# A 2048-wide trunk on one core: the whole down product of the MLP by seven-product slabs, its halves taking turns on the PSUM banks

## The chip, the core and the metric

The kernel runs on one core of a Trainium2 chip. The core has a matrix engine (TensorE, PE in the profile, with its weight loads shown as PEld), three elementwise engines (VectorE = DVE, ScalarE = ACT, GpSimd = POOL) and a queue engine for transfers (SyncE = SP). They run side by side and wait for each other only through semaphores. The metric is device time in microseconds (us) for one execution; the number of a kernel is the median of its timed runs.

## The reference

Two decoder layers over 256 tokens of width 2048, all in float32. What this change touches is the MLP that ends each layer, with `w_ff1` 2048 x 8192 and `w_ff2` 8192 x 2048:

```python
def squared_relu_mlp(h, w1, w2):
    z = jax.nn.relu(h @ w1)
    return (z * z) @ w2

# in each of the two layers, after the attention part
x = x + squared_relu_mlp(rms_norm(x, ffn_norm[i]), w_ff1[i], w_ff2[i])
```

Before the first MLP stand a pooling mixer and a memory attention, between the two MLPs the shared keys and values and a differential attention. None of that is changed.

## The kernel before

**Numbers.** A float32 factor is split in two parts that TensorE multiplies at full rate: a high part (ScalarE rounds, "cast") and a low part (VectorE subtracts the high part from the number). A product takes high x high, high x low and low x high. Weights are read from DRAM in rows of 128 x 1024 numbers (`raw`, `slab`), and every row has to go through one cast on ScalarE (L171) and one subtraction on VectorE (L174) before TensorE may use it. The split parts stand in a ring of six places of 512 columns (`hi_ring`, `lo_ring`), with two more in the MLP (`slot`); a place is free again when TensorE has used it. `Feed` does this: at each use it prepares up to `AHEAD = 3` jobs further, as far as places are free (`fill`, `_slots`).

**Plain tiles.** The up product has 64 output tiles of 128 columns ("f 0" to "f 63"), each summed over 16 blocks of K. `narrow` runs one: per block a 512-column matmul with the weights' high part (L893) and a 256-column one with the low part (L895). Two weight rows feed one tile. `up_tile` copies the finished bank to SBUF (L907), and after every second tile `convert` makes the squared-ReLU pair: eight small steps on VectorE and ScalarE, each put some quarter tiles later by `at(d, fn)`. The results are z (high and low part) and four sums and differences of z's blocks, all kept in `za` and `zb`.

**Slabs.** The second half of the down product's columns (1024 to 2047) isn't run by tiles. For each pair of K blocks, `slab_jobs(i)` runs a 2 x 2 block product with seven products in place of eight. A slab reads two rows (`ra`, `rb`; VectorE also makes one difference, L202, and one sum over 1024 columns, L205; a GpSimd transfer adds a third piece to `ra` while it lands, L142). It is split in four jobs of 2, 1, 2 and 2 products; a product is three 512-column matmuls (L977 to L979) into a PSUM bank of its own. So a slab has 21 matmuls, and the seven sums stay open in seven of the eight banks over all 32 slabs of a layer. Meanwhile all plain tiles use the one bank left (`x_bank`). When the last slab is done, `finish_banks` combines the seven banks into four blocks (two copies on ScalarE, seven additions on VectorE, L999 to L1007), scales them (L1010) and turns them with 16 transposes of TensorE (L1019).

**The first half** of the down product's columns (0 to 1023) runs by plain tiles ("d q n": quarter q of K, column block n), 32 per layer, each with three VectorE steps after it (`add_down`, L913 to L915).

**Order.** `tiles` lists the plain tiles; `slab_plan` puts slab jobs into the gaps between them, one slab to about three gaps. Then a scheduler orders each engine's instructions.

Of the kernel before, what the change touches and what calls it, by code (L numbers as in the profile page):

```python
# [18 lines left out]
P = 128  # L19
T = 256  # L20
# [8 lines left out]
DOWN = 36  # L29
# [254 lines left out]
def slab_plan(tiles):  # L284
# [11 lines left out]
    gaps = {}  # L296
    t = ready[0]
    for i in range(32):
        t = max(t, ready[i])
        groups = ((0,), (1, 2), (3,))  # L300
        late = i - sum(ready[k] <= t for k in ready)
        if late < -2 or t > len(tiles) - 12:
            groups = ((0, 1), (2, 3))
        if tiles[t] == ("d", 3, 0):
            groups = ((0, 1, 2, 3),)
        for g in groups:
            gaps[t] = [(i, j) for j in g]
            t += 1
    return gaps
# [27 lines left out]
def program(ctx, tc, plan, dry, xT, memT, par, lam, cst, wst, yT):  # L337
# [6 lines left out]
    pp = ctx.enter_context(tc.tile_pool(name="pp", bufs=1, space=PSUM))  # L344

# [46 lines left out]
    resid = sp.tile([P, NK, T], F32, name="resid")  # L392
# [411 lines left out]
    def ffn(l, xs, tag, done):  # L804

        ZS, SS = 22, 5
# [12 lines left out]
        made = [-1]  # L819
        whole = [0]  # L820
        ran = [0]
        downs = [0]

        def zs(j, n=1):
            s = j % ZS
            t, s = (za, s) if s < NK else (zb, s - NK)
            return t[:, s : s + n, :]

        def z(j):
            return zs(j)[:, 0, :]  # L830

        def sit(i):
            s = ZS - NK + 2 * (i % SS)
            return zb[:, s : s + 2, :].rearrange("p a c -> p (a c)")
# [4 lines left out]
        def convert(i, late):  # L839
# [16 lines left out]
            def high():  # L856
                assert dry or (2 * i < ZS or downs[0] >= 8 * ((2 * i + 1 - ZS) // NK + 1)), i
                nc.scalar.copy(zs(2 * i, 2)[:, :, 0:T], u)

            def low():  # L860
                whole[0] = 2 * i + 2
                zz = zs(2 * i, 2)
# [9 lines left out]
            def sums_high():  # L872
                assert dry or ran[0] > i - SS, i
                nc.scalar.copy(sit(i)[:, 0:512].rearrange("p (a c) -> p a c", a=2), sums)

            def sums_low():
                h, l = (sit(i)[:, c : c + 512].rearrange("p (a c) -> p a c", a=2) for c in (0, 512))
                nc.vector.tensor_sub(l, sums, h.bitcast(F32))
                made[0] = i
# [5 lines left out]
        def narrow(ps, w, n, ks, src):  # L885
            for j in range(0, len(ks), 2):
# [4 lines left out]
                assert dry or w == "w_ff1" or whole[0] > ks[j + 1]  # L891
# [9 lines left out]
        def up_tile(j, ps):  # L901
# [6 lines left out]
            if j % 2:  # L908
                convert(j // 2, (1, 1, 2, 2, 3, 4, 5, 6) if j == 63 else (1, 2, 3, 4, 6, 7, 8, 10))
# [7 lines left out]
        def down_tile(q, n, ps):  # L917
            ks = list(range(q * NK, q * NK + NK))
            if l == 1 and q == 3 and n == 7:
# [11 lines left out]
                tick()  # L931
                rest = douts[(downs[0] + 1) % 2][:, 0:T]
# [4 lines left out]
            narrow(ps, "w_ff2", n, ks, z)  # L937
            dout = douts[downs[0] % 2]
# [731 lines left out]
```

## Time and profile before

| | |
|---|---|
| timed runs | 2038.71 us median of 3 (2038.3 to 2039.28) |
| the profiled execution's own time | 2039.43 us, span of the profile 2037.7 us |
| PE / PEld busy | 2031.2 us (100%) / 1746.1 us (86%) |
| DVE / ACT / POOL busy | 1626.4 us (80%) / 1322.8 us (65%) / 109.8 us (5%) |
| granted TensorE clock | 1.000 over the whole span |
| HBM | 201 GB/s on average |
| MLP of layer 0, of layer 1 | about 255 to 943 us, about 1341 to 2033 us of the span |

A row of the page's groups reads: line, engine, operation, output<-inputs, sizes, count | busy time, mean duration of one | idle time before it and who ended it. In the timeline a row is start, duration, engine, line and operation; matmuls overlap, so what one costs is the distance from one start to the next.

### The profile page before, as it was taken

The numbers are of one execution on the slowest core, as the hardware profiler recorded it, in microseconds if no ns is written. First come the engines' busy times: TensorE is split into PE (matmuls) and PEld (weight loads), VectorE is DVE, ScalarE is ACT, GpSimd is POOL, SyncE is SP. The second block draws the span as 40 slices with busy tenths as digits, with TensorE's granted clock in tenths as the row PEclk, the third lists the DMA queues.
The fourth block names the chain that finished last, engine by engine and source line by source line (L and its number), as shares of the span: only waits on it lengthen the run. The fifth ranks groups of instructions, "written<-read, shape, count | busy, mean of one in ns | idle before, by whom it ended". The sixth has DMA issues, their size and how long they took to land.

```text
span 2037.7 us, 30955 instructions
## 1 busy us (share of the span) xinstructions
PE 2031.2 (100%) x11088; PEld 1746.1 (86%) x11088; DVE 1626.4 (80%) x2529; ACT 1322.8 (65%) x2105; POOL 109.8 (5%) x131
## 2 busy tenths in 40 slices
PE   9999999999999999999999999999999999999999
PEld 7888888888888888888888899888888888888887
DVE  8888778877877777789775798877877777787787
ACT  7765566666655656669665698566666656665664
POOL 0001300000000000000000000310000000000000
PEclk9999999999999999999999999999999999999999
DMA  9565666776766666766656645657676766667764
GB/s 310 177 201 190 195 191 200 209 222 198 217 210 198 216 203 202 216 186 205 210 186 191 193 142 177 193 174 216 203 222 200 217 198 207 216 198 213 209 203 145
DMA packets 121835, 410.48 MB, mean 201 GB/s; under 512 B 13840, under 2 KB 16912, under 8 KB 121680
## 3 DMA queue, kind: packets, MB, share of 16 engines
q1 hardware_dynamic: 112320, 391.70, 59.6%
q0 software_dynamic: 9216, 16.78, 5.0%
q8 instruction: 87, 1.43, 0.3%
q14 instruction: 68, 0.56, 0.1%
q10 hardware_dynamic: 144, 0.01, 0.0%
HBM read 403.59 MB, written 2.10 MB: 199 GB/s over the span
## 4 chain that ended last, share of the span: by engine, by line
PE 99%; DMA 0%; DVE 0%; SPq 0%; ACT 0%; issue 0%; ACTq 0%
PE x_bank L893 32%; PE x_bank L895 16%; PE wo L488 6%; PE p L978 5%; PE p L977 5%; PE p L979 5%; PE ff L893 3%; PE wo L490 3%; PE q L519 3%; PE k L519 3%; PE v L519 3%; PE u L488 2%; PE mk L519 2%; PE mv L519 2%; PE ff L895 2%; PE u L490 1%
## 5 line engine op out<-in xcount | busy, mean ns | idle before, releaser
L171 ACT CAST hi_ring<-raw 128x512 fp32r<-128x512 f32 (+1 forms) x725 | 575.3, 799 | 351.3 <-PE x_bank L893 146.4
L174 DVE TENSOR_TENSOR lo_ring<-raw,hi_ring 128x512 fp32r<-128x512 f32 (+1 forms) x725 | 659.2, 917 | 173.4 <-ACT hi_ring L171 161.1
L174 DVE TENSOR_TENSOR lo_ring<-slab,hi_ring 128x1024 fp32r<-128x1024 f32 (+1 forms) x182 | 188.1, 1033 | 62.8 <-ACT hi_ring L171 53.7
L171 ACT CAST hi_ring<-slab 128x1024 fp32r<-128x1024 f32 (+1 forms) x182 | 163.9, 901 | 82.2 <-PE x_bank L893 43.5
L893 PE MATMUL x_bank<-fx,hi_ring 128*128 128x512 f32 x688 | 216.1, 395 | 0.0
L488 PE MATMUL wo<-cat,hi_ring 128*128 128x512 f32 x512 | 161.6, 396 | 0.0
L171 ACT CAST slot<-raw 128x1024 fp32r<-128x1024 f32 x84 | 88.3, 1051 | 106.5 <-PE x_bank L893 101.8
L895 PEld LDWEIGHTS x_bank<-fx,lo_ring 128*128 128x128 f32 x688 | 129.2, 188 | 30.2
L142 POOL DMA_DIRECT2D slab<-in_w x64 | 55.4, 865 | 1724.3 <-DMA slab<-in_w 1546.8
L174 DVE TENSOR_TENSOR slot<-raw,slot 128x1024 fp32r<-128x1024 f32 x84 | 103.2, 1229 | 51.1 <-ACT slot L171 51.0
L895 PE MATMUL x_bank<-fx,lo_ring 128*128 128x256 f32 x688 | 135.1, 278 | 0.0
L174 DVE TENSOR_TENSOR slot<-slab,slot 128x1024 fp32r<-128x1024 f32 x74 | 90.5, 1223 | 49.8 <-ACT slot L171 47.9
L893 PE MATMUL x_bank<-fx0a,hi_ring 128*128 128x512 f32 x368 | 115.7, 396 | 0.0
L490 PEld LDWEIGHTS wo<-cat,lo_ring 128*128 128x128 f32 x512 | 96.1, 188 | 22.0
L893 PEld LDWEIGHTS x_bank<-fx,hi_ring 128*128 128x128 f32 x688 | 107.6, 189 | 4.8 <-ACT room L907 1.6
L171 ACT CAST slot<-slab 128x1024 fp32r<-128x1024 f32 x74 | 77.8, 1051 | 50.2 <-PE x_bank L893 31.2
L490 PE MATMUL wo<-cat,lo_ring 128*128 128x256 f32 x512 | 101.7, 278 | 0.0
L893 PE MATMUL x_bank<-fx0b,hi_ring 128*128 128x512 f32 x320 | 100.5, 395 | 0.0
L893 PE MATMUL x_bank<-za,hi_ring 128*128 128x512 f32 x296 | 93.0, 395 | 0.0
L907 ACT COPY room<-x_bank 128x512 f32<-128x512 f32 x118 | 68.7, 582 | 35.9 <-PE x_bank L895 35.9
L895 PEld LDWEIGHTS x_bank<-fx0a,lo_ring 128*128 128x128 f32 x368 | 69.1, 188 | 16.0
L978 PE MATMUL p<-hi_ring,zb 128*128 128x512 f32 x210 | 82.1, 391 | 0.0
(494 smaller groups left out, 4836.8 us busy)
## 6 DMA issues: line engine op xcount, KB each, us to landing
raw<-in_w SPq DMA_DIRECT2D x596, 512.0 KB, 4.2
slab<-in_w SPq DMA_DIRECT2D x128, 512.0 KB, 3.4
slab<-in_w POOLq DMA_DIRECT2D x64, 256.0 KB, 4.8
resid<-in_x SPq DMA_DIRECT2D x8, 256.0 KB, 5.7
memraw<-in_mem SPq DMA_DIRECT2D x4, 512.0 KB, 3.7
out_y<-resid SPq DMA_DIRECT2D x16, 128.0 KB, 1.9
memraw<-in_mem SPq DMA_DIRECT2D x6, 256.0 KB, 6.2
qodd<-both SPq DMA_DIRECT2D x6, 256.0 KB, 3.5
```

The lines of the kernel that those rows point to most:

```text
L142: self.nc.gpsimd.dma_start(t[:, 512:1024], self.wst[other, :, 512:1024], accum_op=ALU.add)
L171: cast = self.nc.scalar.copy(hi, src)
L174: self.nc.vector.tensor_sub(lo, src, hi.bitcast(F32))
L488: nc.tensor.matmul(ps, hi, xs[:, k, :], start=first and j == 0, stop=False)
L490: nc.tensor.matmul(ps[:, T : 2 * T], lo, xs[:, k, 0:T], start=False, stop=last and j == len(ks) - 1,)
L519: nc.tensor.matmul(ps[t], a, b, start=i == 0 and j == 0, stop=i == NK - 1 and j == 2)
L893: nc.tensor.matmul(ps, hi, src(k), start=k == ks[0], stop=False)
L895: nc.tensor.matmul(ps[:, T : 2 * T], lo, src(k)[:, 0:T], start=False, stop=k == ks[-1])
L907: nc.scalar.copy(pairs[j // 2 % 3][:, 512 * (j % 2) : 512 * (j % 2) + 512], ps)
L977: nc.tensor.matmul(ps, al, hi[:, s], start=i == 0, stop=False)
L978: nc.tensor.matmul(ps, ah, hi[:, s], start=False, stop=False)
L979: nc.tensor.matmul(ps, ah, lo[:, s], start=False, stop=i == 31)
```

## The change

Both halves of the down product's columns now go through slabs. Half "A" is the old one (columns 1024 to 2047, all 32 slabs). Half "B" (columns 0 to 1023) takes the first 24 slabs, three quarters of K; the last quarter stays with the eight tiles "d 3 n". The tiles "d 0 n" to "d 2 n" are gone. Seven banks can hold only one half at a time, so the halves take turns: A slabs 0 to 6, B 0 to 13, A 7 to 20, B 14 to 23, A 21 to 31 (`PHASES`). At each turn `finish_banks` combines the seven banks; a sum that isn't whole is parked in a DRAM tile (`part`) and added back at the half's next turn by an accumulating transfer on GpSimd's queue. `ffn_plan` gives each tile credit for four slab jobs. z and its sums get their places from a list (`spots`), since both halves must have read a place before it is free. The second half of the residual stream is copied to a DRAM tile (`kept`) during the MLP, so that its SBUF could serve as two more places; the built program has no instruction that uses these.

```diff
+STEPS = (1, 2, 3, 4, 6, 7, 8, 10)
+NB = 24
+PHASES = (("A", 0, 7), ("B", 0, 14), ("A", 7, 21), ("B", 14, 24), ("A", 21, 32))
+RATE = 4.0
...
+def ffn_plan(tiles):
...
+    jobs = [(p, i, j) for p, (_, a, b) in enumerate(PHASES) for i in range(a, b) for j in range(4)]
+    items = []
+    credit = 0.0
+    phase = hold = 0
+    for t, what in enumerate(tiles):
+        credit = min(credit + RATE, 8.0)
+        if what == ("d", 3, 0):
+            credit = max(credit, 4.0)
+        while t >= hold and jobs and credit >= 1 and ready[jobs[0][1]] <= t:
+            p, i, j = jobs[0]
+            if p != phase:
+                items.append(("end", phase))
+                phase = p
+                hold = t + (4 if PHASES[p - 1][2] == NB else 1)
+                break
+            items.append(("s", *jobs.pop(0)))
+            credit -= 1
+            if not jobs:
+                items.append(("end", phase))
+        items.append(what)
...
+    dp = ctx.enter_context(tc.tile_pool(name="dp", bufs=1, space=bass.MemoryType.DRAM))
...
+        spots = [x[:, 2 * j : 2 * j + 2, :] for x in (za, zb) for j in range(8)]
+        kept = dp.tile([P, NK // 2, T], F32, tag="kept", name=f"kept{l}")
+        nc.sync.dma_start(kept, resid.parts[1])
...
             half, begin, end = PHASES[p]
             n = feed.slab(
-                [[("w_ff2", l, 2 * i + k, c, 4) for c in (2, 3)] for k in range(2)]
+                [
+                    [("w_ff2", l, 2 * i + k, c + 2 * (half == "A"), 4) for c in range(2)]
+                    for k in range(2)
+                ]
             )
...
-                    nc.tensor.matmul(ps, al, hi[:, s], start=i == 0, stop=False)
+                    nc.tensor.matmul(ps, al, hi[:, s], start=i == begin, stop=False)
...
+        def finish_banks(p):
...
+            nc.scalar.copy(x0, p1)
+            nc.scalar.copy(x1, p5)
+            sub(x2, x0, p6)
+            add(x3, x2, p7)
+            add(x0, x0, p2)
+            add(x2, x2, x1)
+            add(x2, x2, p3)
+            add(x1, x1, x3)
+            add(x3, x3, p4)
+            whole = end == (32 if half == "A" else NB)
+            sides = ((x0, 0), (x2, 1), (low, slice(2, 4)))
+            if begin:
+                for side, c in sides:
+                    nc.gpsimd.dma_start(side, part[half][:, c, :], accum_op=ALU.add)
+            if not whole:
+                part[half] = dp.tile([P, 4, 512], F32, tag=f"part{half}{begin}", name=f"part{l}{p}")
+                for side, c in sides:
+                    nc.gpsimd.dma_start(part[half][:, c, :], side)
+                return
...
+            at(8, scale)
             for h in range(4):
-                at(8 + h, lambda h=h: turn(h))
+                at(10 + h, lambda h=h: turn(h))
...
-        tiles = [("f", j) for j in range(NK)]
-        for q in range(3):
-            n = 0
-            for j in range(NK):
-                tiles.append(("f", NK * q + NK + j))
-                for _ in range((0, 2, 2, 1, 1, 1, 1)[j] if j < 7 else 0):
-                    tiles.append(("d", q, n))
-                    n += 1
-        ups = len(tiles)
-        tiles += [("d", 3, n) for n in range(8)]
-        gaps = slab_plan(tiles)
+        tiles = [("f", j) for j in range(4 * NK)] + [("d", 3, n) for n in range(8)]
+        items = ffn_plan(tiles)
```

In the new kernel the splits of L171 and L174 stand at L170 and L173, L202 and L205 at L201 and L204, a pair's conversion at L876 to L906, a slab's matmuls at L1010 to L1012, the combining at L1043 to L1051.

**VectorE in the thick of the MLP.** Before, in layer 0 (`raw` rows feed tiles, `slab` rows feed slabs, `room` is the conversion's workspace):

```order
L205 TENSOR_TENSOR slab176_4539<-slab175_4487,slab176_4539 128x1024
L174 TENSOR_TENSOR lo_ring_75<-raw181_4624,hi_ring_74 128x1024
L174 TENSOR_TENSOR lo_ring_75<-raw182_4638,hi_ring_74 128x1024
L848 TENSOR_TENSOR room0_2621<-room0_2621 128x2x256
L174 TENSOR_TENSOR lo_ring_75<-slab176_4539,hi_ring_74 128x1024
L174 TENSOR_TENSOR slot0_2622<-raw185_4739,slot0_2622 128x1024
L866 TENSOR_TENSOR room0_2621<-room0_2621 128x128
L863 TENSOR_TENSOR za0_2619<-room0_2621,za0_2619 128x2x256
L867 TENSOR_TENSOR room0_2621<-room0_2621 128x256
L174 TENSOR_TENSOR lo_ring_75<-raw186_4755,hi_ring_74 128x1024
L870 TENSOR_TENSOR room0_2621<-room0_2621 128x128
L174 TENSOR_TENSOR lo_ring_75<-slab183_4661,hi_ring_74 128x1024
```

and now, in the same layer, while half B is on the banks:

```order
L173 TENSOR_TENSOR slot0_2625<-raw153_4011,slot0_2625 128x1024
L906 TENSOR_TENSOR za0_2622<-room0_2624,za0_2622 128x512
L173 TENSOR_TENSOR lo_ring_77<-raw154_4076,hi_ring_76 128x1024
L173 TENSOR_TENSOR lo_ring_77<-slab151_3995,hi_ring_76 128x1024
L201 TENSOR_TENSOR slab151_3995<-slab151_3995 128x512
L173 TENSOR_TENSOR slot0_2625<-slab152_4001,slot0_2625 128x1024
L173 TENSOR_TENSOR lo_ring_77<-slab151_3995,hi_ring_76 128x512
L204 TENSOR_TENSOR slab152_4001<-slab151_3995,slab152_4001 128x1024
L876 TENSOR_TENSOR room0_2624<-room0_2624 128x2x256
L173 TENSOR_TENSOR lo_ring_77<-slab152_4001,hi_ring_76 128x1024
L173 TENSOR_TENSOR lo_ring_77<-raw157_4094,hi_ring_76 128x1024
L173 TENSOR_TENSOR lo_ring_77<-raw158_4159,hi_ring_76 128x1024
```

Every tile (two raw rows) is now followed by a whole slab (four splits, L201 and L204), where before one slab was spread over three tiles.

**VectorE at a hand-over of the banks.** Layer 0, from the end of A's slab 6 on (`c_x`, `c_y` and `room` take the combined blocks, slabs 133 and 134 are B's slab 0, slab 137 begins B's slab 1, raw136 is the second row of the tile between them); nothing of the kind stood before in the middle of an MLP:

```order
L173 TENSOR_TENSOR lo_ring_77<-raw136_3686,hi_ring_76 128x1024
L1046 TENSOR_TENSOR room0_2624<-c_y_3716,p1_2892 128x512
L1047 TENSOR_TENSOR c_x_3715<-c_x_3715,p3_2894 128x512
L1048 TENSOR_TENSOR c_y_3716<-c_y_3716,room0_2624 128x512
L173 TENSOR_TENSOR lo_ring_77<-slab133_3575,hi_ring_76 128x1024
L1049 TENSOR_TENSOR c_y_3716<-c_y_3716,p4_2895 128x512
L1050 TENSOR_TENSOR room0_2624<-room0_2624 128x512
L201 TENSOR_TENSOR slab133_3575<-slab133_3575 128x512
L1051 TENSOR_TENSOR room0_2624<-room0_2624,p5_2896 128x512
L173 TENSOR_TENSOR slot0_2625<-slab134_3585,slot0_2625 128x1024
L173 TENSOR_TENSOR lo_ring_77<-slab133_3575,hi_ring_76 128x512
L204 TENSOR_TENSOR slab134_3585<-slab133_3575,slab134_3585 128x1024
```

The combining stands between the splits that the next tile and the next half's first slab need. Behind these rows come the first split of B's slab 1, a conversion step and the last split of B's slab 0. TensorE has one tile between the two halves and then two slabs in a row. The hand-overs after B's slab 13 and A's slab 20 look the same; after B's slab 23 four tiles follow without a slab.

**GpSimd's queue at the hand-over from A to B in mid-MLP** (slabs 245 and 249 begin B's slabs 14 and 15, slab 251 its slab 16):

```order
L141 DMA slab245_5943<-in_w 128x512
L141 DMA slab249_6056<-in_w 128x512
L1056 DMA c_x_6083<-part00_3726 128x512
L1056 DMA c_y_6084<-part00_3726 128x512
L1060 DMA part02_6097<-c_x_6083 128x512
L1056 DMA room0_2624<-part00_3726 128x1024
L1060 DMA part02_6097<-c_y_6084 128x512
L1060 DMA part02_6097<-room0_2624 128x1024
L141 DMA slab251_6072<-in_w 128x512
```

The parked sums are added and written between the accumulating loads of the slabs; before, this queue had nothing but those loads in the MLP.

More of the change, by code (lines that the diff above doesn't have):

```diff
@@ L295, in slab_plan @@
             ready[what[1] // 2] = t + LAG
[L296 to L309, printed above, removed]
+    jobs = [(p, i, j) for p, (_, a, b) in enumerate(PHASES) for i in range(a, b) for j in range(4)]
[18 more added lines that the diff above has]
+        items.append(what)
+    assert not jobs
+    return items
 class Halves:
@@ L937, in down_tile @@
             narrow(ps, "w_ff2", n, ks, z)
+            for i in range(24, 32):
+                left(i, "N")
             dout = douts[downs[0] % 2]
@@ L1053, in go @@
-                if t >= len(tiles) - 3:
+                    if (p, i, j) == (4, 29, 3):
+                        assert {16, 17} <= set(spare)
+                        resid.parts[1] = sp.tile(
+                            [P, NK // 2, T], F32, tag="residb", name=f"resid_b{l}"
+                        )
+                        nc.sync.dma_start(resid.parts[1], kept)
+                    continue
+                if what[0] == "end":
+                    finish_banks(what[1])
+                    ends[0] = True
+                    continue
```

159 lines of the change are left out of this document (89 added, 70 removed).

## The prediction

> **What bounds the kernel now.** I read the page's busy table first, then its chain of waits, then the waits of TensorE, then the two MLPs by windows.
>
> ```profile
> span 2037.7 us, 30955 instructions
> PE 2031.2 (100%) x11088; PEld 1746.1 (86%) x11088; DVE 1626.4 (80%) x2529; ACT 1322.8 (65%) x2105; POOL 109.8 (5%) x131
> PE 99%; DMA 0%; DVE 0%; SPq 0%; ACT 0%; issue 0%; ACTq 0%
> ```
>
> The chain that ended last is TensorE from beginning to end: no other engine has a share above half a per cent. In the list of who waited for whom TensorE has three entries in 2037.7 us, the longest 1.1 us, all at the start.
>
> ```profile
> 255.00:943.00 688.00, 688.00 (x3744) 589.87 (x3743) 550.49 (x702) 445.05 (x583) 26.33 (x31) 1.00 0.67 205
> 1341.00:2033.00 692.00, 692.00 (x3771) 593.45 (x3769) 546.50 (x690) 434.98 (x555) 28.22 (x32) 1.00 0.66 203
> 885.00:912.00 27.00, 27.00 (x143) 23.09 (x142) 25.25 (x36) 20.49 (x28) 0.86 (x1) 1.00 0.69 205
> ```
>
> These are stages by windows: stage, its length, busy time of PE, PEld, DVE, ACT, POOL, then granted clock, DMA share and GB/s. In both MLPs TensorE never pauses, at clock 1.00, and VectorE is busy 80% and 79%. The third row, where slabs stand thickest today, shows VectorE at 25.25 of 27 us (94%) with TensorE still unbroken. So a matmul removed is time gained, as long as VectorE keeps up.
>
> **What the change removes.** Matmuls overlap, so I take distances between starts, from the timeline of TensorE around the one place where a whole slab stands between two tiles:
>
> ```profile
> 878.31 0.62 PE L893 MATMUL x_bank<-fx0a,slot 128*128 128x512 f32 x2
> 883.88 0.40 PE L977 MATMUL p<-hi_ring,za 128*128 128x512 f32 x1
> 887.74 0.39 PE L979 MATMUL p<-lo_ring,za 128*128 128x512 f32 x1
> 888.64 0.61 PE L893 MATMUL x_bank<-za,hi_ring 128*128 128x512 f32 x2
> ```
>
> A tile is 883.88 - 878.31 = 5.57 us, a slab 888.64 - 883.88 = 4.76 us. Both do 16 blocks of K x 128 columns' worth of work. Per layer 24 "d" tiles become 24 slabs, so 48 x 0.81 = **38.9 us less** on TensorE. The removed tiles' copies and three VectorE steps each were hidden beside it and give nothing themselves.
>
> **What it adds on TensorE.** Half B has to be turned too, 16 transposes per layer. They start 0.11 us apart:
>
> ```profile
> 931.60 0.27 PE L1019 MATMUL ct<-const,c_b 128*128 128x128 f32 x1
> 931.71 0.27 PE L1019 MATMUL ct<-const,c_a 128*128 128x128 f32 x1
> ```
>
> 32 x 0.11 = **+3.5 us**.
>
> **VectorE in an even stretch.** From its timeline, again by distances:
>
> ```profile
> 875.20 1.22 DVE L174 TENSOR_TENSOR lo_ring<-slab,hi_ring 128x1024 fp32r<-128x1024 f32 x1
> 876.34 0.28 DVE L866 TENSOR_TENSOR room<-room 128x128 f32<-128x128 f32 x1
> 876.66 0.42 DVE L867 TENSOR_TENSOR room<-room 128x256 f32<-128x256 f32 x1
> 877.00 1.22 DVE L174 TENSOR_TENSOR lo_ring<-raw,hi_ring 128x1024 fp32r<-128x1024 f32 x1
> 878.14 0.28 DVE L870 TENSOR_TENSOR room<-room 128x128 f32<-128x128 f32 x1
> 878.34 1.22 DVE L174 TENSOR_TENSOR lo_ring<-slab,hi_ring 128x1024 fp32r<-128x1024 f32 x1
> 879.47 0.68 DVE L878 TENSOR_TENSOR zb<-room,zb 128x512 fp32r<-128x512 f32 x1
> 880.08 0.68 DVE L202 TENSOR_TENSOR slab<-slab 128x512 f32<-128x512 f32 x1
> 882.47 1.22 DVE L174 TENSOR_TENSOR slot<-slab,slot 128x1024 fp32r<-128x1024 f32 x1 [0.26 <-ACT slot L171]
> 883.73 1.22 DVE L205 TENSOR_TENSOR slab<-slab,slab 128x1024 f32<-128x1024 f32 x1
> 886.13 1.23 DVE L174 TENSOR_TENSOR lo_ring<-slab,hi_ring 128x1024 fp32r<-128x1024 f32 x1 [0.57 <-ACT hi_ring L171]
> ```
>
> 1024 columns occupy VectorE for 1.14 us, 512 for 0.61, the three small conversion steps for 0.32, 0.34 and 0.20. A tile needs two splits, 2.28. A slab needs three wide splits, one of 512, L202 and L205: 4 x 1.14 + 2 x 0.61 = 5.78. A conversion is 3 x 0.61 + 0.86 = 2.69 per two tiles. A round of one tile and one slab, which is now the rule, takes VectorE 9.41 us against TensorE's 5.57 + 4.76 = 10.33: 91%, which the 94% window bears. Throughput is no bound there, so the order within a round decides.
>
> In a round the last to be ready is the low part for the slab's fourth job. Its chain begins when the tile's first weight row leaves its place (2.78 us into the tile): cast, split, split, L205, cast, split. TensorE asks for it at 5.57 + (887.74 - 883.88) = 9.43 us, so there are 6.65 us. Today's whole slab ran that chain in 5.97 us, from the cast at 881.39 to the split's end at 887.36, 0.38 us before its use.
>
> ```profile
> 881.39 1.04 ACT L171 CAST slot<-slab 128x1024 fp32r<-128x1024 f32 x1
> 885.04 1.05 ACT L171 CAST hi_ring<-slab 128x1024 fp32r<-128x1024 f32 x1 [0.38 <-DVE slab L205]
> ```
>
> In the new order it is cast 1.05, split 1.14, the 512 split 0.61, L205 1.22, cast 1.05, split 1.22: 6.3 us. It fits by some 0.3 us. I count **+2 us** for all of them, with 0 below and, at 0.3 us lost in each of the 78 even rounds (39 of a layer's 56 slabs), 23 above.
>
> **The hand-overs.** Three times in a layer (after A6, B13, A20) the seven banks are combined while TensorE has a single tile, and then come two slabs in a row. Let T be the last slab's end. From there VectorE has, without a break, the tile's second split 1.14, six combining steps of 0.61, the next slab 5.78, the first split of the slab behind it 1.14 and a conversion step 0.61: 12.3 us. TensorE wants the last of it at T + 9.4. It can run the second slab's first products meanwhile (1.4 us, and the order shows them moved up), so 1.5 of these 2.9 us stand. Then a load binds: B's third slab gets its buffer when that split is done.
>
> ```profile
> slab<-in_w SPq DMA_DIRECT2D x128, 512.0 KB, 3.4
> slab<-in_w POOLq DMA_DIRECT2D x64, 256.0 KB, 4.8
> L142 POOL DMA_DIRECT2D slab<-in_w x64: 853/862/1005, 88.7 to 1979.8; - x64
> DMA to landing us min/median/max: 3.6/4.8/6.7
> ```
>
> Load 3.4, accumulating load 4.8, cast 1.05, split 1.22: T + 22.8, against a use at 5.57 + 9.52 + 5.57 + 0.46 = 21.1. Following the printed rows with these durations, place by place, I get 3.9 us of waiting per hand-over. The count of VectorE against the following tile's second half alone gives 0.4 (18.7 against 18.3); all waits added, 2.9 + 1.7 = 4.6. I take 3.3, nearer the walk, since its rows are in the trace: 6 x 3.3 = **+19.8 us** (bounds 2 and 28).
>
> **Smaller terms.** After A's last slab three accumulating transfers must land before the scaling and the turn, which stand two and a half tiles later (T + 13.9). VectorE ends the combining near T + 7.1; the last transfer is 512 KB, no such row exists; with 4.8 to 6.7 of the 256 KB rows and the scaling's 0.72 the blocks are ready at 12.7 to 14.6, a little later for twice the bytes: **+3 us** for both layers (0 to 8). After B's last slab two tiles follow each other on `x_bank` and the second waits for the copy (0.58, and ScalarE's current cast): **+2** (1 to 3).
>
> ```profile
> L907 ACT COPY room<-x_bank 128x512 f32<-128x512 f32 x118 | 68.7, 582 | 35.9 <-PE x_bank L895 35.9
> PEld x_bank L893 <- ACT room L907: 6.7, 30, 0.2
> L1010 ACT ACTIVATE c_b<-c_b,d_x x4: 719/722/724, 920.1 to 2014.1; 128x512 f32<-128x512 f32 x4
> ```
>
> Elsewhere a slab job stands between two tiles, as today, where the wait is at most 0.2 us and hidden behind the running matmul. The copies to `kept` and back (1 MB each) are issued early in the MLP on SP's queue, with the next four rows already loaded: 0.
>
> The page "Perfetto Trace Analysis" of the Trainium skill (section "Optimizing Tensor Performance", Matmuls) asks that independent matmul groups rotate through PSUM banks. This change speaks against it, since the tiles have one bank nearly throughout. By that rule alone the nine places per layer where the plan puts tile behind tile would each wait about 1 us, +18 in place of +2. The scheduler's order puts six slab matmuls between them at eight of the nine, so I keep +2.
>
> **Sum.** -38.9 + 3.5 + 2 + 19.8 + 3 + 2 = -8.6. Against the profiled execution's own 2039.43 us (span 2037.7 and 1.7 around it) that is 2030.8; the median of the shown runs lies 0.7 lower: **2030 us**.
>
> **The rivals.**
>
> *The hand-overs hide.* For it: TensorE's order there is interleaved, and lead gained before T could swallow most. Against: the ring holds eight places, four jobs at most. At 0.7 us each: 2030 - 6 x 2.6 = 2014.
>
> *VectorE's chain paces the even rounds (slower than before).* Place: the fourth job of each slab; mechanism: freed place, cast, split, split, sum, cast, split. It decides from 6.65 us on, and 0.1 us more costs 7.8 us over 78 rounds; from 0.13 us over it takes the gain away. For it: the margin is 0.3 us, and ScalarE's bank copy and two conversion steps can stand before either cast (0.5 each). Against: today's 0.38 us to spare. At 0.3 over: 2030 - 2 + 23 = 2051.
>
> *GpSimd's queue holds the slabs.* At A20 to B14 six transfers of parked sums, three of which wait for another to land (4.8), stand before the accumulating load of B16. By the rows they end near T + 14, and that load can't start before its first part has landed at T + 15.8, so it is not late; with landings of 6.7 the queue is free only near T + 17, a us or two late. If at all six hand-overs 2 us are lost so: 2042.
>
> *VectorE holds GpSimd's descriptors.* A busier VectorE would lengthen L142 beyond 853/862/1005 ns. If each transfer on that queue came 1.2 us later (one wide VectorE step), the even rounds have some 6 us of slack and only the hand-overs pay: 2030 + 6 x 1.2 = 2037. The Trainium skill, page "SBUF — State Buffer", section "SBUF: two separate sides", warns that VectorE's two-port modes keep GpSimd from writing descriptors. This trace doesn't show it: 1005 ns is the longest of 64 issues, with VectorE at 80%.
>
> **How the numbers follow.** Forecast 44%, with its own range 2021 to 2040; hand-overs hidden 18%; even rounds paced by VectorE 26%; GpSimd's queue 8%; descriptors 4%. About 0.2% (4 us) is what a measurement of this kernel can tell from no change. Faster than 2034.6: 18 and some 31 of the 44, 0.49. Slower than 2042.8: 26 and a third of the queue's 8, with 2 of the forecast's, 0.31. Within: 0.20. The range that leaves out two in ten reaches from below the first rival to the second: 2011 to 2052.
>
> **What would show it.** In the changed kernel's page: PE's busy time near 1995 us, VectorE near 1780 us (88%; 48 slabs x 5.78, less 48 tiles x 3.4, and eight more combinings). TensorE's waits: about 20 us for `lo_ring` or `hi_ring` in six clusters of 3 to 4 us behind A6, B13 and A20; few and short ones in between; `ct` or its scaling some 1.5 us twice. If waits of 0.1 to 0.4 us recur at every L1012 of a fourth job, the chain paced it. If L141 lands late behind L1056 and L1060, it was GpSimd's queue. Wrong altogether would be a tile or slab that itself takes longer than 5.57 or 4.76 us without a wait.

## The result: slower, 2090.7 us against 2038.9

The changed kernel takes 2090.73 us in the median (2087.09 to 2094.42, 4 runs), the kernel before 2038.93 (median of four runs; the table ahead of the prediction has the first three): a ratio of 1.0254, 95% interval 1.0235 to 1.0274. Forecast were 2030 us with a range of 2011 to 2052. The profiled execution took 2087.09 us. From its page: the span, TensorE's and VectorE's busy time, and the shares of the chain that ended last.

```profile
span 2085.2 us, 30357 instructions
PE 2031.4 (97%) x10592; PEld 1713.7 (82%) x10592; DVE 1771.7 (85%) x2641; ACT 1373.1 (66%) x2177; POOL 178.8 (9%) x215
PE 86%; DMA 5%; DVE 5%; ACT 2%; issue 2%; POOL 0%; DVEq 0%; ACTq 0%; POOLq 0%; SPq 0%
```

TensorE has 496 matmuls fewer (11088 before) and is as long busy as before (2031.2). The chain, TensorE from end to end before, now runs through transfers and VectorE as well. TensorE's waits, longest in total first (what waited, for what: us in all, times, longest):

```profile
PE p L1010 <- ACT slot L170: 23.8, 12, 5.6
PE ct L1076 <- DVE resida L1079: 8.9, 2, 4.6
PE ct L1076 <- ACT c_b L1067: 6.0, 2, 4.5
PE p L1010 <- ACT hi_ring L170: 3.7, 13, 0.4
PE p L1012 <- DVE lo_ring L173: 3.2, 7, 0.6
PE p L1012 <- DVE slot L173: 2.1, 4, 0.5
```

The table of the first layer by windows shows where they are (stage, its length, busy time of PE, PEld, DVE, ACT, POOL, then granted clock, DMA share, GB/s): the even rounds of B's first run, the hand-overs behind A6 and A20, B's end, A's end.

```profile
420.00:540.00 120.00, 120.00 (x618) 101.93 (x617) 110.44 (x131) 82.60 (x106) 11.38 (x14) 1.00 0.79 230
391.00:414.00 23.00, 18.36 (x81) 13.31 (x80) 17.91 (x21) 13.41 (x16) 1.77 (x2) 1.00 0.60 179
685.00:735.00 50.00, 42.66 (x193) 33.20 (x192) 39.58 (x50) 27.13 (x34) 7.85 (x10) 0.93 0.69 197
800.00:835.00 35.00, 30.52 (x170) 26.18 (x170) 26.48 (x37) 20.52 (x30) 3.46 (x4) 0.95 0.67 202
943.00:966.00 23.00, 18.52 (x105) 16.06 (x104) 17.29 (x29) 13.85 (x25) 2.60 (x3) 0.93 0.84 243
```

In the even rounds TensorE does not pause in 120 us, with VectorE at 92%. Each of the other four windows has TensorE idle for 4.5 to 7.3 us, and three of them a granted clock below 1. Before, no 25 us of the MLPs had either. TensorE's timeline behind the longest wait:

```profile
717.67 0.80 PE L1010 MATMUL p<-slot,za 128*128 128x512 f32 x1 [5.60 <-ACT slot L170]
719.52 0.63 PE L1010 MATMUL p<-slot,za 128*128 128x512 f32 x1
719.95 0.63 PE L1011 MATMUL p<-slot,za 128*128 128x512 f32 x1
```

The same place by windows, columns as above:

```profile
717.70:723.30 5.60, 5.56 (x11) 3.29 (x12) 5.60 (x7) 3.44 (x5) 0.34 (x1) 0.50 0.28 48
723.40:729.00 5.60, 5.60 (x29) 4.60 (x28) 4.72 (x6) 4.02 (x5) 0.00 (x0) 1.00 0.83 256
```

Matmuls at clock 0.50 start 0.43 us apart in place of 0.23, and count as busy all the while; that is about half of why the busy time did not fall. The record of the granted clock has eight such stretches, each 3.41 or 6.83 us long, 37.5 us together (a mean of 0.991 over the span). They cost up to half their length, some 18 us.

To see every stage at once I took from the starts of the matmuls how long each stage lasted beyond its tiles (5.565 us), slabs (21 x 0.2268) and transposes (0.11). Both layers together, us; the stages are named by the up tiles they begin and end with:

```
                      f0-16  f17-21  f22-30  f31-36  f37-44  f45-50  f51-54  f55-59  f60-d4  d5-end   sum
                      (A0-6) behind  (B)     behind  (A)     behind  (B)     B's     (A)     A's
                             A6              B13             A20             end             end
changed                4.9    13.6    0.8     18.5    0.8     25.5    1.4     14.9     2.9     7.1   90.2
no parking             4.8    10.8    0.9     20.7    0.8     18.9    1.3      2.2     4.3    -0.6   64.0
five rows, own         5.2     2.3    0.6      2.3    0.8      4.4    2.9     12.6     2.2     9.9   43.0
five rows, sums early  5.0     2.3    0.6      2.3    1.0      4.3    2.3      2.1     2.2    -0.2   21.9
three rows, sums early 5.2    14.2    0.7     17.0    0.7     29.1    1.7      2.1     7.7    -0.5   77.8
four rows, sums early  5.2    13.8    0.7     14.5    0.7     26.5    5.2      3.7     2.3     0.3   72.8
no double slab         4.8     5.9   14.5      9.4   16.4     21.9   10.4     17.4    15.5    10.3  126.4
double slab later      4.9     5.4    8.8      6.6    6.5     21.5    6.6     14.7     3.7    13.8   92.3
five rows, no double   5.1     2.4    0.7      2.1    0.8      2.1    3.3      5.9     4.5     0.2   27.1
before: 7.0 in both layers together
```

The change: 48 x (5.565 - 4.763) = 38.5 saved, 3.5 of transposes, 90.2 - 7.0 = 83.2 lost, together 48.2; the two profiled executions differ by 47.7. Of the 90.2 the six hand-overs hold 57.7, B's ends 14.9, A's ends 7.1.

Split at the same starts, the 57.7 us are 32.2 of listed waits (0.15 us and longer), 12.2 of matmuls at half clock and 13.2 of smaller pieces between one start and the next. Over all stages the smaller pieces come to some 24 us, against 7.0 before; they count as busy for the most part and are the other half of why the busy time did not fall.

### The profile page after: what moved, and what is told of

The parts are those of the page before. It is cut to its first block, busy times and chain, and to the rows that moved or that the text cites. A ratio compares the mean times of both kernels' runs of the same rounds, so it can differ in the third digit from the quotient of the medians.

```text
span 2085.2 us, 30357 instructions
## 1 busy us (share of the span) xinstructions
PE 2031.4 (97%) x10592; PEld 1713.7 (82%) x10592; DVE 1771.7 (85%) x2641; ACT 1373.1 (66%) x2177; POOL 178.8 (9%) x215
## 4 chain that ended last, share of the span: by engine, by line
PE 86%; DMA 5%; DVE 5%; ACT 2%; issue 2%; POOL 0%; DVEq 0%; ACTq 0%; POOLq 0%; SPq 0%
PE x_bank L919 19%; PE x_bank L921 9%; PE p L1012 7%; PE p L1010 7%; PE p L1011 7%; PE wo L503 6%; DMA slab<-in_w 3%; PE ff L919 3%; PE wo L505 3%; PE k L534 3%; PE v L534 3%; PE q L534 3%; PE u L503 2%; PE mk L534 2%; PE mv L534 2%
## 5 line engine op out<-in xcount | busy, mean ns | idle before, releaser
L173 DVE TENSOR_TENSOR lo_ring<-raw,hi_ring 128x512 fp32r<-128x512 f32 (+1 forms) x643 | 555.0, 879 | 108.2 <-ACT hi_ring L170 99.8
L170 ACT CAST hi_ring<-raw 128x512 fp32r<-128x512 f32 (+1 forms) x643 | 482.8, 766 | 202.8 <-PE wo L503 62.7
L170 ACT CAST hi_ring<-slab 128x1024 fp32r<-128x1024 f32 (+1 forms) x336 | 304.4, 906 | 135.6 <-DVE slab L204 60.9
L173 DVE TENSOR_TENSOR lo_ring<-slab,hi_ring 128x1024 fp32r<-128x1024 f32 (+1 forms) x336 | 346.9, 1043 | 44.2 <-ACT hi_ring L170 42.0
L141 POOL DMA_DIRECT2D slab<-in_w x112 | 97.2, 868 | 1655.5 <-DMA slab<-in_w 700.6
L170 ACT CAST slot<-slab 128x1024 fp32r<-128x1024 f32 x112 | 117.4, 1049 | 159.4 <-PE x_bank L919 109.4
L173 DVE TENSOR_TENSOR slot<-slab,slot 128x1024 fp32r<-128x1024 f32 x112 | 137.0, 1223 | 86.2 <-ACT slot L170 86.0
L204 DVE TENSOR_TENSOR slab<-slab,slab 128x1024 f32<-128x1024 f32 x112 | 136.5, 1219 | 0.2
L173 DVE TENSOR_TENSOR slot<-raw,slot 128x1024 fp32r<-128x1024 f32 x70 | 85.5, 1222 | 19.7 <-ACT slot L170 19.5
L921 PEld LDWEIGHTS x_bank<-fx0b,lo_ring 128*128 128x128 f32 x448 | 84.2, 188 | 19.9
L1010 PE MATMUL p<-hi_ring,zb 128*128 128x512 f32 x230 | 91.0, 396 | 1.1 <-ACT hi_ring L170 0.9
L1011 PE MATMUL p<-hi_ring,zb 128*128 128x512 f32 x230 | 89.9, 391 | 0.0
L1012 PE MATMUL p<-lo_ring,zb 128*128 128x512 f32 x230 | 89.0, 390 | 0.0
```

The lines of the kernel that those rows point to most:

```text
L141: self.nc.gpsimd.dma_start(t[:, 512:1024], self.wst[other, :, 512:1024], accum_op=ALU.add)
L170: cast = self.nc.scalar.copy(hi, src)
L173: self.nc.vector.tensor_sub(lo, src, hi.bitcast(F32))
L204: add(two, t.unsqueeze(1).to_broadcast([P, 2, 512]), two)
L921: nc.tensor.matmul(ps[:, T : 2 * T], lo, src(k)[:, 0:T], start=False, stop=k == ks[-1])
L1010: nc.tensor.matmul(ps, al, hi[:, s], start=i == begin, stop=False)
```

## What binds at a hand-over: two theories

The chain of waits behind A6 and behind A20 (start, us, what):

```profile
394.12 3.36 DMA slab<-in_w
398.12 7.40 DMA slab<-in_w
405.59 1.05 ACT slot L170
700.98 7.30 DMA slab<-in_w
708.92 7.58 DMA slab<-in_w
716.57 1.05 ACT slot L170
```

It is the same both times: VectorE gives up a slab's row, the third slab's plain load gets it, GpSimd's accumulating load follows, ScalarE casts, TensorE goes on. T, the start of the tile behind the last slab, is 381.96 and 688.80 in TensorE's timeline, so the row is free and the load starts at T + 12.2 both times. The theory **buffers**: the three rows, held by the double slab and the combining, make the loads late. The theory **traffic**: the parked sums, on GpSimd's queue and on the DMA engines, make them late. At A20 GpSimd's timeline seems to speak for traffic:

```profile
698.83 0.90 POOL L1056 DMA_DIRECT2D room<-part  x1
707.11 0.55 POOL L1060 DMA_DIRECT2D part<-room  x1 [6.81 <-DMA room<-part]
708.92 0.89 POOL L141 DMA_DIRECT2D slab<-in_w  x1 [1.26 <-DVE lo_ring L173]
```

But the queue stood idle for 1.26 us ahead of the last row. In the chain above, the plain load landed only at 708.28 (700.98 + 7.30), and the accumulating one follows it. So it was not the queue's order that held the slab here, but a slow plain load.

### No parked sums

```
             if begin:
-                for side, c in sides:
-                    nc.gpsimd.dma_start(side, part[half][:, c, :], accum_op=ALU.add)
...
             if not whole:
-                part[half] = dp.tile([P, 4, 512], F32, ...)
-                for side, c in sides:
-                    nc.gpsimd.dma_start(part[half][:, c, :], side)
                 return
```

> The changed kernel without its parked sums: no transfer to or from DRAM at a hand-over or an end, so what the earlier runs of a half summed is dropped from the output. All else stays, the double slab behind each hand-over too. The changed kernel lost about 52 us at its six hand-overs (waits, and TensorE at half clock behind the long ones) and about 22 us at its four ends. If the parked transfers hold the slabs' loads (theory 'traffic'), the hand-overs behind A6, B13 and A20 fall below 3 us each and the ends to nothing: 2090 - 35 - 22 = about 2033. If it is the double slab with its three row buffers (theory 'buffers'), the hand-overs behind A6 and B13 keep their 6 to 8 us each, only A20's excess over them (about 4 each) and the ends go: 2090 - 8 - 20 = about 2062.

Measured: 2058.33 us, ratio to before 1.0093 (1.0078 to 1.0108). The waits for the slot, 23.8 us before, are 15.0 here. The chain behind A20 in this run:

```profile
700.38 3.52 DMA slab<-in_w
704.51 7.74 DMA slab<-in_w
```

So the parked transfers cost 32 us by the medians (26 between the two profiled executions, on which the table rests), but mostly at the ends (22.0 to 1.6 in the table). The hand-overs keep 50.4 of 57.7. At A20 the plain load lands in 3.52 in place of 7.30 without them. The accumulating load takes 7.74 all the same: it runs while the feed's ordinary loads run. "Traffic" alone is refuted; "buffers", with 2062, fits.

### Five row buffers for slabs

```
-t = self.rows.tile([P, 1024], F32, tag="rows", bufs=3, name=f"slab{h}")
+k = self.nslab % 5
+self.nslab += 1
+if self.spare is not None and k > 2:
+    t = self.spare[:, k - 3, :]          # in the place of `more`
+else:
+    t = self.rows.tile([P, 1024], F32, tag="rows", bufs=3, name=f"slab{h}")
```

> The changed kernel with five row buffers for slabs in place of three; the two more lie in the place that the change frees when it copies half of the residual to DRAM. The double slab and the parked transfers stay. Theory 'buffers': the third slab's load no longer waits for a row, its waits go, and only VectorE's 12.3 us of work against 9.4 stand, 1.5 to 3 us per hand-over: about 2090 - 52 + 6 x 3 = 2055. Theory 'traffic': GpSimd's accumulating load still stands behind the parked transfers and waits stay above 4 us at A20: 2075 or more.

Measured: 2045.62 us, ratio 1.0031 (1.0021 to 1.0040), nine below the 2055 of 'buffers'. In this run some rows in the freed place were written again before their last reader, so it computed with wrong weights and only its time counts. The next gave each row a tile of its own (tags `residb0` and `residb1`, the second half of the residual cut into two parts to match). In both runs the two more rows are given back at A's slab 27, and the residual's copy comes back after A's last slab, two slabs later than in the changed kernel.

> As the run with five row buffers, but each row in the freed place is a buffer of its own, so that no row is written before its last reader (in the earlier run some were, so its numbers stood for its time only). All transfers, the double slab and the output are those of the changed kernel. Theory 'buffers': the same time as there, 2040 to 2050, no wait above 1.5 us at a hand-over, and what is left is the waits at the ends (some 16 us) with their half-clock stretches. If the earlier run was fast only since rows were overwritten early, the waits of 3 to 6 us for the slot of the third slab come back: 2075 or more.

Measured: 2040.89 us, ratio 1.0006 (0.9997 to 1.0016). Its waits of TensorE:

```profile
PE ct L1096 <- ACT c_b L1087: 8.0, 2, 4.5
PE ct L1096 <- DVE resida L1099: 7.3, 2, 4.4
PE p L1030 <- ACT hi_ring L176: 0.6, 2, 0.3
PE p L1032 <- DVE lo_ring L179: 0.4, 1, 0.4
```

Of the slabs' 32.8 us of waiting 1.0 is left. The combining, the double slab and the parked transfers are all still there, and the loads land as slowly as before: at A20 the accumulating load took 7.68 us. It only was for a slab further ahead. The rows are the cause at the hand-overs, and VectorE's 12.3 us of work there costs TensorE next to nothing. What the six places still lose in the table (9.0) is mostly not waiting. It goes in pieces of about 0.1 to 0.3 us, many of them where TensorE's order changes between tile and slab; what makes them isn't shown.

### The double slab: taken out, and moved

```
-RATE = 4.0
+RATE = 4.2
...
                 hold = t + (4 if PHASES[p - 1][2] == NB else 1)
+                credit = credit if PHASES[p - 1][2] == NB else 0.0
```

> The changed kernel with one slab in place of two behind A6, B13 and A20; the slab that is left over is spread over the later gaps of the same run as single jobs (rate 4.2), so every hand-over stands behind the same tile as before. Parked transfers stay. Theory 'buffers': the waits for the slot of the third slab (23.8 us in all) fall below 5 us, TensorE's half-clock stretches go with them, the six hand-overs shrink from 52 to about 12 us: about 2050. Theory 'traffic': the waits stay within a few us, 2080 or more. If the even rounds were the bound after all, the extra jobs in them would show as waits of 0.1 to 0.5 us at L1012.

Measured: 2124.64 us, ratio 1.0421 (1.0404 to 1.0439): neither theory, 34 us worse than the change. The hand-overs shrink (57.7 to 37.2), but the even rounds lose 41 us where they lost 3. By the plan only every fifth round has a fifth job, but from the first of these on each slab is cut: its first job or two stand behind one tile, the others behind the next. TensorE's waits:

```profile
PE p L1011 <- ACT hi_ring L170: 18.6, 20, 4.7
PE p L1013 <- DVE lo_ring L173: 13.0, 30, 0.7
PE x_bank L922 <- DVE lo_ring L173: 7.4, 12, 0.7
```

That looked like the rival of the prediction in which VectorE's chain paces the even rounds. The other variant keeps the jobs of a slab together and moves the double slab back:

```
                 hold = t + (4 if PHASES[p - 1][2] == NB else 1)
+                if PHASES[p - 1][2] != NB:
+                    credit, twice = 0.0, t + 6
...
-        credit = min(credit + RATE, 8.0)
+        credit = min(credit + RATE * (1 + (t == twice)), 8.0)
```

> The changed kernel, three row buffers, with the double slab moved from directly behind A6, B13 and A20 to five tiles later; single slabs behind the hand-over. Theory 'it takes the combining and the double slab together': without the combining's 3.7 us VectorE frees the rows by T + 19.1 where TensorE needs the third slab at T + 21.1, so the waits for its slot (23.8 us) nearly go, the ends stay: about 2040 to 2050. Theory 'a double slab alone outruns three rows': the waits move five tiles back and keep most of their size: 2070 to 2090.

Measured: 2088.85 us, ratio 1.0238 (1.0223 to 1.0253). A miss for the first theory in its total. Behind A6 and B13 the loss falls from 32.1 to 12.0, the runs in which the double slab now stands rise from 3.0 to 21.9, and A20, with its parked sums read and written, keeps 21.5. The plain load of the chain there, beside the parked sums:

```profile
695.86 10.05 DMA slab<-in_w
```

So a double slab outruns three rows in the even rounds too, and at A20 the parked transfers seem to be enough without one (no run took both away). It doesn't do so everywhere: behind B23 the plan sets a double slab as well, after four tiles without one, and where no sums are waited for there (no parking, or three rows with the sums early) that stage loses 2.1 or 2.2 us in both layers together. Whether the loss of the run with no double slab was VectorE's chain or the rows was told by giving it five rows (and the early sums of the next section):

> The run with five rows and the sums brought early (2019.4 us), with the single slab behind the hand-overs and the left-over slab spread job by job (as in the run without a double slab, 2124.6). It tells why that run lost. Theory 'rows': there too the slabs' loads came late, so with five rows the waits for hi_ring and lo_ring of single jobs go and the time is 2015 to 2022. Theory 'order of the jobs': a fifth job in a round outruns VectorE's chain of cast, split, sum, cast and split, whatever rows there are; then the waits of 0.4 to 0.7 us at the fourth job (30 of them there, 13 us) and those for hi_ring stay for the most part: 2040 or more.

Measured: 2026.47 us, ratio 0.9938 (0.9923 to 0.9953). The even rounds are back at 4.8 us for both layers, and the waits for the ring are gone:

```profile
PE p L1031 <- ACT slot L176: 3.5, 7, 0.7
PE x_bank L942 <- DVE lo_ring L179: 1.2, 3, 0.7
```

It was the rows there, too; VectorE's chain bears a cut slab, and a fifth job in every fifth round, when its data are there. The 2026 miss the expected 2015 to 2022: A's last run, with its single jobs, loses 4.5 and B's end 5.9.

## The ends, and a version that beats both

The chain behind B's last slab and behind A's last (start, us, what), in the changed kernel:

```profile
809.93 8.63 DMA room<-part
949.82 8.78 DMA c_b<-part
```

Both accumulate 512 KB from DRAM, and scaling and turn wait for them. So (the two freed rows are given back at B's slab 19 for this, and taken again behind B's end):

```
+if (p, i, j) in ((3, 22, 0), (4, 30, 0)):       # B's, A's last slabs but one
+    to = ...      # B: the two freed rows; A: two idle parts of the room
+    for c in range(2):
+        nc.sync.dma_start(to[c], part[half][:, 2 * c : 2 * c + 2, :])
...
-if begin:
+if whole:
+    add(x0, x0, early...); add(x2, x2, early...); add(low, low, early[1])
+elif begin:
     for side, c in sides:
         nc.gpsimd.dma_start(side, part[half][:, c, :], accum_op=ALU.add)
```

> The five rows, and at the two ends of a layer the parked sums are brought back by plain loads on SP's queue one or two slabs before the end (into the freed rows for B, into idle parts of the room for A) and added by VectorE (0.61 + 0.61 + 1.14 us), in place of accumulating transfers on GpSimd's queue behind the combining. Theory 'the landing of the accumulating transfers (8.6 to 8.8 us) makes the ends wait': the waits of 8.5 and 7.3 us at the transposes go, and the half-clock stretches behind them (20.5 us at half the clock): about 2045 - 16 - 8 = 2021. If instead VectorE's combining or the bank for the turn makes them wait, 2 to 4 us stay at each of the four ends: 2032 or more.

Measured: 2019.44 us, ratio 0.9898 (0.9881 to 0.9914): faster than before by 1.0%, than the change by 3.4%. In a span of 2019.4 us TensorE's waits, one more of 1.1 us at the program's start aside, are down to these and two of 0.3 and 0.2:

```profile
PE ff L939 <- ACT hi_ring L176: 1.4, 2, 0.9
PE mk L554 <- ACT hi_ring L176: 1.3, 1, 1.3
PE p L1032 <- DVE lo_ring L179: 0.4, 1, 0.4
```

The clock is 1.0 to the last microseconds. With -38.5 + 3.5 + (21.9 - 7.0) = -20.1 the sum of the prediction comes out at last (2019.44 - 2039.63 = -20.2).

The run with the sums early but three rows tells whether the two repairs add up, and with four how much lead is needed:

> The sums brought early at the ends as in the run of 2019.4 us, but with the three row buffers of the changed kernel (the freed place then holds only the sums brought back). It tells whether ends and hand-overs add up. The changed kernel's loss beyond its tiles and slabs was some 58 us at the hand-overs and some 22 us at the ends; if they are separate, the hand-overs keep their waits for the slot (23.8 us in all) and half-clock stretches and only the ends' part goes: 2090.7 - 21 = about 2070. If the transfers at the ends also delayed later hand-overs, 2060 or less.

Measured: 2075.89 us, ratio 1.0177 (1.0161 to 1.0194). That is 6 us above the forecast. Ends and hand-overs are separate for the most part: 14.8 us gained here on the change, 49.8 by the rows (2090.73 - 2040.89), 64.6 in all, and 71.3 by both; the ends' 22.0 fall to 1.6, and part of that is lost again behind A20 and in A's last run.

> One size changed: four row buffers, between the runs with three (2075.9 us) and five (2019.4 us) that bring the sums early. With three, the third slab's first row behind a hand-over follows the second row of the first slab, which VectorE gives up 12.2 us behind the last slab's end; with four it follows that slab's first row, given up some 3 us earlier (its last reader is the sum at L204, 390.00 to 391.22 in the changed kernel's first hand-over, against 394.09). Theory 'each us that the row is free earlier is a us less of waiting, and of half clock behind it': 6 x 3 us of waiting and most of the 31 us at half clock go (12 to 15 us): about 2045. Theory 'what counts is a whole slab of lead': little changes, 2065 or more.

Measured: 2067.68 us, ratio 1.0131 (1.0114 to 1.0148), near the second theory and a miss for mine. Behind A6 the row does come free 2.9 us earlier (T = 384.08, the load at 393.42, so T + 9.3 in place of 12.2). But TensorE's order changed too: it now has this slab's first products 18 matmuls into the second tile in place of behind it (the scheduler seems to count on the earlier row), and there TensorE waits again, in its timeline:

```profile
405.02 0.50 PE L1030 MATMUL p<-slot,za 128*128 128x512 f32 x1 [3.17 <-ACT slot L176]
```

And in the list of its waits:

```profile
PE p L1030 <- ACT slot L176: 31.5, 6, 9.5
```

Six hand-overs, six waits. A microsecond of lead was not a microsecond of waiting less here. That the order took it up fits these rows, but no run held the order fixed; five rows ended it.

## What a pause costs

The kernel before, with pauses put in by a matmul whose data go through two or three small transfers:

```
+GATES = {6: 2, 10: 3, 24: 2, 28: 3, 38: 2, 42: 3, 52: 2, 56: 3}
...
 nc.scalar.copy(pairs[...], ps)               # up tile j leaves its bank
+if j in GATES:
+    g = pairs[...][:, ... + 8]
+    for n in range(GATES[j]):
+        to = cp.tile([P, 8], F32, ...); nc.scalar.dma_start(to, g); g = to
...                                           # ahead of the next up tile:
+nc.tensor.matmul(ps[:, 0:2], ones_d, g[:, 0:2], start=True, stop=True)
```

> The kernel before, with 16 pauses of TensorE (8 per layer): ahead of a tile stands a small matmul that needs data which has gone from the last tile through two or three transfers one after the other. By the rows (copy 0.58, a small transfer 2 to 2.5 us each, covered by 2.4 us of slab work on average) a pause is 3 us with two transfers and 5.5 with three, about 68 us in all. Theory 'a pause costs its length': time = 2039 + the sum of the waits in the trace, granted clock 1.0. Theory 'a pause also lowers the clock': behind each pause of 3 us and more stands a stretch of 3.4 or 6.8 us at clock 0.5, which costs 1.7 to 3.4 us more: some 25 us beyond the sum of the waits.

Measured: 2156.15 us, 117 above before. TensorE's waits are 79.9 us (2.1 before), so some 39 us went beyond them (37 in the profiled execution); the expected 25 was too little. Three of the pauses:

```profile
343.65 0.35 PE L905 MATMUL x_bank<-gate,ones_d 128*128 128x2 f32 x2 [1.80 <-DMA gate<-gate]
512.74 0.35 PE L905 MATMUL x_bank<-gate,ones_d 128*128 128x2 f32 x2 [3.54 <-DMA gate<-gate]
551.22 0.56 PE L905 MATMUL x_bank<-gate,ones_d 128*128 128x2 f32 x2 [6.60 <-DMA gate<-gate]
```

The record of the granted clock has half-clock stretches of 3.41, 6.83 or 10.24 us, 58 us in all, at all eight gates that waited 3.54 us or longer (one more gate shows a stretch without a wait put down to it, and one shows neither), and none at the six that waited 0.49 to 2.13. That half clock is up to 29 of the 39 us; the rest is not traced. The Trainium skill ("TensorE: Matmul & The Clock Gate", Part 1, "What's actually happening") has the clock halved after an idle window of about 3.4 us. The stretches agree, as multiples of 3.41. But no whole idle window was needed here: behind B13 of the second layer of the changed kernel waits of 1.28 and 0.53 us were enough, and behind A6 of the first 2.16 and 0.53 us were not.

The record of the granted clock shows what made the difference. Within one execution all stretches begin on one grid of 3.41 us. I cut each execution's span into these windows and summed TensorE's idle time in each (the first 30 and last 8 us left out). In the nine profiled executions that have such stretches inside, all 52 windows at full clock with 1.80 us idle or more are followed by half clock, and of those with 1.76 or less a single one (1.60). The 1.28 and 0.53 us fell into one window, 1.81 us in all; the 2.16 and 0.53 us into two, with 1.35 and 1.49 idle. So what counted was the idle time summed within a window, from about half of it on, and not one long wait.

## Why the prediction failed, step by step

**Right.** The 38.9 saved (38.5 by the matmuls' starts). The even rounds: 2 us forecast, 3.0 lost in their three runs; the chain of 6.3 in 6.65 us fits with that. VectorE's busy time (1780 forecast, 1771.7). VectorE's 12.3 us of work at a hand-over: the row came free at T + 12.2. That tiles one after the other on one bank hardly wait: no wait of a matmul for the bank's copy stands in the list, and the 18 us by the rule on banks did not come. VectorE does not hold up GpSimd's descriptors; the issue of the accumulating load is as long as before, with VectorE at 85%:

```profile
L141 POOL DMA_DIRECT2D slab<-in_w x112: 857/866/1008, 87.5 to 2037.0; - x112
DMA to landing us min/median/max: 3.5/4.8/9.3
```

**Wrong: the hand-overs, 19.8 us forecast and 57.7 measured.** The step that failed is "Load 3.4, accumulating load 4.8, cast 1.05, split 1.22: T + 22.8". The mechanism was named rightly (B's third slab gets its buffer late); its size came from medians over the whole kernel. Behind a hand-over, with several 512 KB loads at work at once, the accumulating load took 7.40 us at A6, 6.96 at B13 and 7.58 at A20, and the plain one 7.30 at A20, where parked sums ran beside it. Another 0.6 us passed at A6 between the first landing and the second load's start (397.48 to 398.12), which the sum left out. The cast thus ended there at T + 24.7 (405.59 + 1.05 - 381.96) and not at T + 21.6, and TensorE had run out before. With 7.40 for 4.8 the walk would have given 6.5 us of waiting and not 3.9, by estimate; the listed waits are 32.2 us, 5.4 per hand-over, most of them for the cast of a `slot` and not for `lo_ring` or `hi_ring`, as "What would show it" had it. The upper bound of 4.6 us had no landing longer than the median in it; the quoted row said 6.7, and even that was too short. Four rows showed that the distance in us does not settle it by itself; five settled it. The other 25 of the 57.7 us had no term at all: 12.2 at half clock and 13.2 in the smaller pieces.

**Missing: the clock.** Every wait was priced at its length. Some 18 us of the 83 are matmuls at half clock behind waits, and the pauses in the old kernel show the same. With some 17 us more of smaller pieces than before, that is why TensorE's busy time is 2031 and not the 1995 of "What would show it".

**Missing: B's end.** The 3 us were for A's end alone (7.1 measured), from landings of 4.8 to 6.7. B23 brings parked sums back in the same way, and nothing stood for it: 14.9 us. The accumulating 512 KB took 8.63 and 8.78 us. The "+2" for B's end was for the bank only.

**Small.** A0 to A6 lose 2.5 us more than the same tiles before (4.9 against 2.4), where each of these slabs now stands as six and fifteen matmuls between tiles, with pieces of 0.1 us at the changes; not foreseen.

**The rivals.** "The hand-overs hide" was right of the mechanism and wrong of this kernel: the ring is not what stops them, three rows are, and with five they hide. "VectorE's chain paces the even rounds" is refuted (120.00 of 120.00 us, and the run with five rows and cut slabs). "GpSimd's queue holds the slabs" is not what bound even at A20, where the queue stood idle before the slab's load. What the parked sums did there was to slow the plain load (7.30 us, 10.05 in the run with the double slab moved, 3.52 without parked sums), and that cost more than the rival's 2 us: in the run with the double slab moved A20 lost 10.3 and 11.1 us in the two layers against 2.3 and 3.1 behind A6.

**Open.** What makes the accumulating loads land in 7 to 8 us there: without the parked sums they still take 6.05, 7.24 and 7.74, beside the feed's own loads. The DMA engines' share during these landings was 0.87, 0.81 and 0.83, little above the 0.79 of the even rounds, so it doesn't explain them by itself. That the loads slow each other is argued, not shown; no run took the other loads away. What the smaller pieces between the starts are made of isn't settled either.

## What to carry to other kernels

Where two units of work follow each other that used to alternate, count the buffers of the loads behind them, and price a load that starts late by the longest landing that the trace shows, or more, and not by the median. Sum TensorE's waits by windows of 3.41 us: where they came to some 1.8 us or more here, they cost their length and up to half of the 3.4 to 10 us behind them. An accumulating transfer on the way to a result was better replaced here by a load that starts before the result exists and an addition on VectorE.

## What was not expected of the hardware

An accumulating read of 512 KB from DRAM took 8.4 us in the median, a plain write of the same blocks on the same queue 3.8:

```profile
part<-room POOLq DMA_DIRECT2D x6, 512.0 KB, 3.8
room<-part POOLq DMA_DIRECT2D x4, 512.0 KB, 8.4
```

The two did not run beside the same loads: one of the writes, at A20 of the first layer, took 6.80 us, and the last accumulating read of the program (`c_b`, 512 KB) 5.94. How much of the 8.4 is the accumulating itself isn't shown.

And busy time is no measure of work done: 496 matmuls fewer kept TensorE busy for as long, in part at half clock.
